# A two-layer decoder trunk on one core: the second plain pair of each gated MLP moves from the opening to the first two chained units

## The chip, the cores and the metric

The kernel runs on 1 core of one Trainium2 chip. The metric is the device time of one execution in microseconds (us); a kernel's time is the median of its runs. Engines are named as in the profile: PE (matmul), DVE (vector), ACT (scalar), POOL and SP. ACT, DVE and PE each work through their own queue in order; SP issues the loads, POOL issues transfers that add one block of SBUF onto another.

## The reference

Two layers over 512 tokens of width 1024, float32. Each layer has a token mixer (a gated recurrence with pooling in layer 0, a convolution module in layer 1), a cross-attention into 256 memory tokens, and the part that the change touches, a gated MLP with a causal depthwise convolution of width 3 on the gate branch:

```python
def conv_ffn(x, norm, w_up, dw_w, dw_b, w_down):
    h = rms_norm(x, norm) @ w_up
    g = causal_dwconv(h[..., :D_FF], dw_w, dw_b)
    u = h[..., D_FF:]
    return (jax.nn.gelu(g) * u) @ w_down
```

D_FF is 3072, so gate and value have 24 blocks of 128 columns each, "pairs" below. A final RMS norm ends the trunk.

## The kernel before, in words

Activations lie transposed: a tile has 128 channels on the partitions and 512 tokens beside them. Every float32 product is made of three matmuls on operands split into a high and a low part (`mm3`, L186 to L188): high on ACT, low on DVE. A weight piece is fetched into `raw` (ring of 3), its high part goes to `whi`, its low part to `wlo`.

The RMS norm isn't applied to x before the product. `norm.x` holds x times the gain, split; the factor of each token, `norm.r`, multiplies the product afterwards. It is one over the root of the mean of squares: `split(norm.ss)` splits the sum of squares, two matmuls (`mean_of`, L287 and L288) sum it over the channels into the bank `stat`, ACT takes the square root (L1037), and DVE the reciprocal (L1040).

The 24 pairs of a layer are made in two ways:

- The first two (`PLAIN = 2`) are plain: a gate chunk and a value chunk, each 24 matmuls of 512 tokens (`start`). `start(0)` and `start(1)` belong to pair 0, `start(2)` and `start(3)` to pair 1. `gate(c)` scales the gate chunk by `norm.r`, applies the convolution (an Identity on ACT with the middle tap, L894, and two taps on DVE, L897) and the Gelu (L899); `values(c)` multiplies by the value chunk and splits the result.
- The other 22 go through `unit(c)` for c = 2 to 23. A unit makes gate and value of one pair from seven products instead of eight of half the size (12 matmuls of 256 tokens each): with weight blocks a11, s1, s2, a12, s3, s4, a22 and operands that are the halves of `norm.x` or their sums T1 to T4. The sums come from `seven.sums(k)`, k = 0 to 3: two scaled copies on ACT (L749), four subtractions on DVE (L755 to L761), four high parts on ACT (L763) and four low parts on DVE (L766). Three of the four are made in the attention before; `sums(3)` is made in the MLP's opening.

Three PSUM accumulators serve a unit. G takes a11; ACT copies G into F (L927, the seed), and G goes on with a12, F with s2, s3 and a22. Between s2 and s3, and between s3 and a22, ACT copies F out to `u` (L946, L960); PE may write F again only after that. H takes s1 and s4. PE's order in a unit is s1, s2, a12, s3, then (from unit 4 on) 24 matmuls of the down projection, then a11 of the next pair (`ahead`), s4 and a22.

The blocks s1 to s4 don't come from memory. They are made in place in `raw` by accumulating transfers that POOL issues once a low part is done: after a11's low part `r += z` (L824), after s3's `z += a22` and `r += a22` (L827), after s2's `r += a12` (L829). The ACT row that makes s3's high part reads what the first of them left.

The order on PE, ACT, DVE and POOL is written out by hand (`manual_schedule`): it is the order of the code in `opening` and `unit`. SP's order comes from the scheduler. In `unit` the line `next(left)` takes one step of what the previous pair left over, between the unit's own steps.

`opening` computes the four plain chunks, the root and the last sums, and prepares the first units; `first` is pair 2, `second` pair 3. The down projection of six groups of four pairs is added to x in `Down`; the first down unit of a layer (c = 4) adds on DVE (`sum`), all later ones seed the bank from x on ACT (L854) and copy it home (L859).

Of the kernel before, what the change touches and what calls it, by code (L numbers as in the profile page):

```python
# [10 lines left out]
F32 = mybir.dt.float32  # L11
F32R = mybir.dt.float32r
AF = mybir.ActivationFunctionType
ALU = mybir.AluOpType
# [47 lines left out]
def trunk(ctx: ExitStack, tc: tile.TileContext, I: dict, out: list):  # L62
# [35 lines left out]
    def main_ps():  # L98
        return psum.tile([P, T], F32, tag="mm", name=nm("mm"))
# [370 lines left out]
    def attention(layer, norm, mem, nxt, six, up):  # L470
# [363 lines left out]
    def ffn(layer, norm, nxt, seven, pairs):  # L834
        ys = {}

        class Down:
# [8 lines left out]
            def products(self, i, ps, seeded=False, ks=range(GC)):  # L846
# [3 lines left out]
            def bank(self, i, seeded):  # L850

                ps = aux_ps()
                if seeded:
                    A.activation(ps, X[2 * self.j + i], AF.Copy)  # L854
                return ps

            def home(self, i, ps, seeded):
                if seeded:
                    A.activation(X[2 * self.j + i], ps, AF.Copy)  # L859
                else:  # L860
                    self.sum(i, ps)

            def sum(self, i, ps):
                n = 2 * self.j + i
# [65 lines left out]
        def unit(c):  # L930

            nonlocal left, chains
            G, F = chains
            down, seeded = downs.get(c), c > GC
# [11 lines left out]
            A.activation(u[:, :M], F, AF.Copy)  # L946
            next(left, None)
            high(c + 1, "a22")

            m(c, G, "a12", seven.B21, False)  # L950
            next(left, None)
            if down:
                d = [down.bank(i, seeded) for i in range(2)]
# [11 lines left out]
            high(c + 1, "a12")  # L965
            low(c + 1, "a12")
            if down:
                for ks in (range(GC - 1), (GC - 1,)):
                    for i in range(2):
                        down.products(i, d[i], seeded, ks)  # L970
            if c + 3 in pairs:
                pairs[c + 3].load()
            if c + 2 in pairs and c > first:
                pairs[c + 2].load_second()
            if c >= GC - 1 and c + 1 in downs:
                downs[c + 1].w.high()
                downs[c + 1].w.low()
            if c + 2 in downs and c + 2 <= CF:
                downs[c + 2].load()
            high(c + 1, "s1")  # L980
            low(c + 1, "s1")
            high(c + 1, "s2")
            low(c + 1, "s2")
            if down:
                down.home(0, d[0], seeded)

            if c + 1 in pairs:
                chains = ahead(c + 1)
            if down:
                down.home(1, d[1], seeded)  # L990
# [4 lines left out]
            next(left)  # L995

        def opening():

            nonlocal left, chains
            ps, y = {}, {}  # L1000

            def start(i, ks=range(C)):
                if ks[0] == 0:
                    ps[i] = main_ps()
                for k in ks:
                    mm3(ps[i], blk(w[0], k * P), norm.x[k], k == 0, k == C - 1)
                if ks[-1] == C - 1:
                    w.pop(0)

            def fetch(i):  # L1010
                w.append(Piece(I["wup"][(layer * 2 + i % 2) * PLAIN + i // 2]))
                w[-1].high()

            def gate(c):
                g = tmp_f()
                V.tensor_tensor(g, ps.pop(2 * c), norm.r, op=ALU.mult)
                for y[c] in gate_conv(c, g):
                    yield
                V.tensor_tensor(y[c], y[c], norm.r, op=ALU.mult)

            def values(c):
                V.tensor_tensor(y[c], ps.pop(2 * c + 1), y[c], op=ALU.mult)
                ys[c] = act_r(), act_r()
                A.activation(ys[c][0], y[c], AF.Copy)

            def close(c):
                V.tensor_tensor(ys[c][1], y[c], ys[c][0].bitcast(F32), op=ALU.subtract)
# [9 lines left out]
            A.activation(root, mean, AF.Sqrt, bias=eps)  # L1037
            A.activation(small.tile([P, 1], F32, tag="warm", name=nm("gelu"), bufs=1), eps, AF.Gelu_apprx_tanh)
            norm.r = small.tile([P, T], F32, tag="r", name=nm("r"), bufs=1)
            V.reciprocal(norm.r, root)  # L1040
# [24 lines left out]
            next(g, None)  # L1065

            start(3)
            chains = ahead(first)

            def rest():  # L1070
                values(1)
                yield
                close(1)

            left = rest()

        left, chains = None, None
        first, second = PLAIN, PLAIN + 1
# [12 lines left out]
        if nxt:  # L1091
            mem = Memory(1)
            mem.operand(0)
            mem.operand(1)
            mem.outputs()
            parked = []
            for n in range(PARKED):
                if n + 1 < C // 2:
                    downs[CF + n + 1].w = load_w(I["wdown"][(layer * NG + NG - 1) * (C // 2) + n + 1])
                parked.append(mem.key_piece(n, park=True))  # L1100
            for j in range(C // 2):
                for i in range(2):
                    ps = mm_ps()
                    downs[CF + j].products(i, ps)
                    downs[CF + j].sum(i, ps)
# [780 lines left out]
```

## Time and profile before

| | |
|---|---|
| runs | 1433.17, 1434.95, 1437.86 us, median 1434.95 |
| profiled execution | 1440.97 us, span 1439.2 us |
| granted clock of PE, mean | 0.997 |
| PE busy | 1421.0 us of the span |
| DVE, ACT, POOL busy | 1079.1, 910.2, 317.4 us |
| opening of layer 0 | first matmul at 356.65 us |
| opening of layer 1 | first matmul at 1045.94 us |

The profiled execution is one run; its own time is the span plus what lies around it. Busy times say how much an engine had to do; what sets the end is found in the waits of the engine that is nearly always busy.

### The profile page before, as it was taken

Reading aid. Unit: us, or ns where it says so; the run is one execution under the profiler, and the core shown is the slowest. Engines: PE = TensorE matmul, PEld = TensorE weight load, DVE = VectorE, ACT = ScalarE, POOL = GpSimd, SP = SyncE. Lnnn points to the kernel's source line nnn. Section 1 sums busy time; section 2 is a strip of 40 time slices with the busy share of each in tenths; the row PEclk is TensorE's granted clock in tenths of the full one; section 3 lists DMA queues with packets and bytes.
Section 4 is the critical chain, followed back from the end, with each engine's and each line's share of the span. In section 5 each row is a group of like instructions: output and inputs, shape, how many; then the busy total and the mean of one; then the engine's idle time right before and its main releaser. Section 6 shows DMA issues by size and latency. Waiting matters only on the chain.

```text
span 1439.2 us, 22840 instructions
## 1 busy us (share of the span) xinstructions
PE 1421.0 (99%) x8650; PEld 1263.3 (88%) x8650; DVE 1079.1 (75%) x1796; ACT 910.2 (63%) x1592; POOL 317.4 (22%) x333
## 2 busy tenths in 40 slices
PE   9999999999999999999999999999998999999998
PEld 8888888988999999999888777899888999999997
DVE  6987776778876666666789997877787666676665
ACT  7668755667556666666655557667654666666664
POOL 0012310100122222222009991011002222222211
PEclk9999999999999999999999999999999999999999
DMA  8522242544487777777432364345438777777751
GB/s 302 194 88 89 88 132 69 118 108 146 115 197 170 173 175 166 170 176 155 133 117 88 118 183 143 92 96 132 116 104 183 175 174 170 164 177 166 164 123 59
DMA packets 80318, 205.36 MB, mean 143 GB/s; under 512 B 9040, under 2 KB 9552, under 8 KB 80208
## 3 DMA queue, kind: packets, MB, share of 16 engines
q1 hardware_dynamic: 51120, 151.20, 34.0%
q0 software_dynamic: 28800, 52.44, 21.4%
q8 instruction: 67, 1.10, 0.3%
q14 instruction: 43, 0.35, 0.1%
q10 hardware_dynamic: 288, 0.27, 0.1%
HBM read 146.21 MB, written 2.10 MB: 103 GB/s over the span
## 4 chain that ended last, share of the span: by engine, by line
PE 82%; issue 6%; DMA 4%; DVE 3%; POOL 2%; ACT 2%; SPq 0%; POOLq 0%; DVEq 0%; ACTq 0%
PE mm L187 19%; PE mm L186 19%; PE mm L188 19%; PE aux L186 7%; PE aux L187 7%; PE aux L188 7%; PE mm L458 2%; DMA raw<-wa 1%; DMA raw<-raw 1%; DMA raw<-in_wv 1%; DMA wa<-in_wpair 1%; DVE wlo L167 1%; POOL actf L1487 1%; POOL act L167 1%; PE aux L532 1%
## 5 line engine op out<-in xcount | busy, mean ns | idle before, releaser
L186 PE MATMUL mm<-act,whi 128*128 128x512 f32 (+2 forms) x1061 | 369.2, 349 | 1.1 <-ACT whi L803 1.1
L187 PE MATMUL mm<-act,whi 128*128 128x512 f32 (+2 forms) x1061 | 369.3, 348 | 0.8 <-DVE act L181 0.4
L188 PE MATMUL mm<-act,wlo 128*128 128x512 f32 (+2 forms) x1061 | 369.0, 348 | 0.0
L186 PEld LDWEIGHTS mm<-act,whi 128*128 128x128 f32 x1061 | 200.5, 189 | 29.2 <-ACT whi L803 1.5
L187 PEld LDWEIGHTS mm<-act,whi 128*128 128x128 f32 x1061 | 200.7, 189 | 28.2 <-DVE act L167 1.0
L188 PEld LDWEIGHTS mm<-act,wlo 128*128 128x128 f32 x1061 | 200.7, 189 | 24.9 <-DVE wlo L167 0.6
L186 PE MATMUL mm<-bigr,bigr 128*128 128x256 f32 x704 | 199.8, 284 | 5.0 <-ACT tmp L946 5.0
L188 PE MATMUL mm<-bigr,bigr 128*128 128x256 f32 x704 | 199.8, 284 | 0.1
L187 PE MATMUL mm<-bigr,bigr 128*128 128x256 f32 x704 | 199.6, 284 | 0.0
L186 PE MATMUL aux<-act,whi 128*128 128x512 f32 x399 | 156.2, 391 | 0.0
L187 PE MATMUL aux<-act,whi 128*128 128x512 f32 x399 | 156.0, 391 | 0.0
L188 PE MATMUL aux<-act,wlo 128*128 128x512 f32 x399 | 155.5, 390 | 0.0
L827 POOL DMA_DIRECT2D raw<-wa x100 | 88.4, 904 | 283.9 <-DVE bigr L821 151.1
L166 ACT ACTIVATE whi<-raw 128x1024 fp32r<-128x1024 f32 (+1 forms) x95 | 96.7, 1022 | 85.9 <-PE mm L187 46.3
L814 ACT ACTIVATE bigr<-raw 128x512 fp32r<-128x512 f32 x176 | 109.5, 624 | 55.1 <-DVE wlo L203 38.5
L186 PEld LDWEIGHTS mm<-bigr,bigr 128*128 128x128 f32 x704 | 135.4, 192 | 5.6 <-ACT tmp L946 5.6
L171 DVE TENSOR_TENSOR tmp<-mm,tmp 128x256 f32<-128x256 f32 x130 | 54.0, 420 | 110.1 <-PE mm L188 109.6
L188 PEld LDWEIGHTS mm<-bigr,bigr 128*128 128x128 f32 x704 | 135.5, 193 | 0.5 <-DVE bigr L821 0.5
L187 PEld LDWEIGHTS mm<-bigr,bigr 128*128 128x128 f32 x704 | 135.4, 192 | 0.0
L821 DVE TENSOR_TENSOR bigr<-raw,bigr 128x512 fp32r<-128x512 f32 x176 | 121.0, 688 | 12.9 <-ACT bigr L814 9.5
L824 POOL DMA_DIRECT2D raw<-raw x50 | 43.3, 867 | 390.5 <-DVE wlo L821 229.8
L167 DVE TENSOR_TENSOR wlo<-raw,whi 128x1024 fp32r<-128x1024 f32 (+1 forms) x75 | 90.4, 1211 | 20.8 <-ACT whi L166 20.3
(353 smaller groups left out, 3067.5 us busy)
## 6 DMA issues: line engine op xcount, KB each, us to landing
raw<-wa POOLq DMA_DIRECT2D x150, 256.0 KB, 4.0
wa<-in_wpair SPq DMA_DIRECT2D x88, 256.0 KB, 3.8
raw<-in_wpair SPq DMA_DIRECT2D x44, 512.0 KB, 3.9
big<-in_wdown SPq DMA_DIRECT2D x44, 512.0 KB, 4.0
raw<-raw POOLq DMA_DIRECT2D x50, 256.0 KB, 5.0
raw<-in_pw SPq DMA_DIRECT2D x24, 512.0 KB, 3.3
raw<-in_win SPq DMA_DIRECT2D x20, 512.0 KB, 3.3
raw<-in_wk SPq DMA_DIRECT2D x16, 512.0 KB, 3.5
```

The lines of the kernel that those rows point to most:

```text
L166: A.activation(hi, src, AF.Copy)
L167: fetched[1] = (eng or V).tensor_tensor(lo, src, hi.bitcast(F32), op=ALU.subtract)
L171: V.tensor_tensor(out, a, b, op=ALU.add)
L186: PE.matmul(ps, wh, xh, start=first, stop=False, skip_group_check=onto)
L187: PE.matmul(ps, wh, xl, start=False, stop=False, skip_group_check=onto)
L188: PE.matmul(ps, wl, xh, start=False, stop=last, skip_group_check=onto)
L458: PE.matmul(p, m[j], x, start=k == 0 and j == 0 and x is hi, stop=k == C - 1 and x is lo)
L532: PE.transpose(pt[:, qc * P : (qc + 1) * P], es[h][qc // 2][:, j : j + P], ident)
L814: A.activation(self.w[name][0], self.block(name), AF.Copy)
L821: V.tensor_tensor(lo, self.block(name), hi.bitcast(F32), op=ALU.subtract)
L824: G.dma_start(self.r, self.z, accum_op=ALU.add)
L827: G.dma_start(block, self.a22, accum_op=ALU.add)
```

## The change

It has five parts, the same in both layers.

- `start(2)` and `start(3)`, the chunks of pair 1, leave the opening. `plain_gate` runs the first of them in unit 2 behind s3, `plain_values` the second in unit 3 behind s3, in the two banks `aux`; the steps of `gate(1)` and `values(1)` stand in these two units and the next.
- The mean's two matmuls stand after six of the eight operands of `start(0)` instead of after `start(0)` and two operands of `start(1)`.
- `seven.sums(3)` stands ahead of the square root, where it stood behind the first steps of `gate(0)`.
- The opening prepares s4 of `first` and a11 of `second`; a22 of `second` and a11 of pair 4 move into the first unit.
- The down projection always seeds its bank, at c = 4 too. One `load()` of the first down block goes, which had been issued twice. In the attention, the splits of a11 and a22 wait for the last score step.

```diff
-        prepare("a11", "a22")
+        with tc.issue_after(score.last):
+            prepare("a11", "a22")
...
-            if c == first:
-                both(c + 2, "a11")
...
             if down:
                 for ks in (range(GC - 1), (GC - 1,)):
                     for i in range(2):
-                        down.products(i, d[i], seeded, ks)
+                        down.products(i, d[i], ks)
+            if plain:
+                next(plain)
...
-            if c + 2 in pairs and c > first:
+            if c + 2 in pairs:
                 pairs[c + 2].load_second()
...
+            if plain:
+                gate1 = next(plain)
+                if c == first:
+                    plains[second] = plain_values(gate1)
...
+        def plain_gate():
+
+            start(2)
+            fetch(3)
+            w[-1].low()
+            yield
+            g = gate(1)
+            next(g)
+            yield g
+
+        def plain_values(g):
+
+            start(3)
+            for _ in g:
+                pass
+            yield
+            for _ in values(1):
+                pass
+            yield
...
             ss = split(norm.ss)
-            start(0)
-            fetch(2)
-            w[-1].low()
-            start(1, range(2))
+            start(0, range(6))
             mean = mean_of(ss)
+            start(0, range(6, C))
+            start(1)
             Norm.due = None
+            for _ in seven.sums(3):
+                pass
             root = tmp_f()
             A.activation(root, mean, AF.Sqrt, bias=eps)
...
             V.reciprocal(norm.r, root)
-            start(1, range(2, C))
+            fetch(2)
             pairs[second].load()
             pairs[second].load_second()
-            fetch(3)
             g = gate(0)
             next(g)
             w[-1].low()
-            pairs[second + 1].load()
-            pairs[second + 1].load_second()
-            downs[GC].load()
-            t = seven.sums(3, lambda: (next(g), next(g)))
-            next(t)
-            next(g, None)
-
-            start(2)
-            both(second, "a11")
-            g = gate(1)
-            next(g)
-            values(0)
-            both(second, "a22")
+            both(first, "s4")
             next(g)
             next(g)
-            next(t, None)
-            close(0)
+            both(second, "a11")
             next(g, None)
-
-            start(3)
+            pairs[second + 1].load()
             chains = ahead(first)
...
+            left = values(0)
```

In the lists below `mm` and `aux` are PSUM banks, `act` split operands, `raw` and `wa` fetched blocks, `whi` and `bigr` high or low parts, `stat` the bank of the mean; line numbers of the changed kernel differ by a few from those above.

PE, first chunk of the opening in layer 0, as a piece of the difference:

```order
 L187 MATMUL mm_700_3566<-act_647_3338,whi_694_3552 128x512
 L188 MATMUL mm_700_3566<-act_646_3337,wlo_695_3553 128x512
+L287 MATMUL stat_701_3585<-act_698_3562,ones_100 128x512
+L288 MATMUL stat_701_3585<-act_699_3563,ones_100 128x512
 L186 MATMUL mm_700_3566<-act_667_3438,whi_694_3552 128x512
 L187 MATMUL mm_700_3566<-act_668_3439,whi_694_3552 128x512
```

The two matmuls of the mean now stand inside the first chunk, behind its 18th matmul.

ACT, from the split of the sum of squares to the root and the Gelu's table, before:

```order
L166 ACTIVATE act_698_3562<-tmp_691_3546 128x512
L200 ACTIVATE whi_702_3593<-raw_701_3591 128x1024
L1037 ACTIVATE tmp_706_3607<-stat_705_3604,eps_85 128x512
L1038 ACT_TABLE_LOAD
L1038 ACTIVATE gelu_707_3609<-eps_85 128x1
```

and the same stretch of the change:

```order
L166 ACTIVATE act_698_3562<-tmp_691_3546 128x512
L750 ACTIVATE tmp_703_3619<-x_91,par_89 128x512
L750 ACTIVATE tmp_704_3620<-x_91,par_89 128x512
L764 ACTIVATE bigr_619_3236<-tmp_705_3623 128x256
L764 ACTIVATE bigr_621_3238<-tmp_706_3624 128x256
L764 ACTIVATE bigr_623_3240<-tmp_705_3623 128x256
L764 ACTIVATE bigr_625_3242<-tmp_706_3624 128x256
L1056 ACTIVATE tmp_707_3637<-stat_701_3585,eps_85 128x512
L1057 ACT_TABLE_LOAD
L1057 ACTIVATE gelu_708_3639<-eps_85 128x1
```

The six rows of the last sums moved ahead of the square root; the split of a fetched piece moved behind it.

ACT, around the first unit's seed (L927 before, L924 in the change) and its first copy to `u` (L946, L941), before:

```order
L814 ACTIVATE whi_726_3698<-raw_709_3631 128x512
L894 ACTIVATE tmp_729_3705<-tmp_728_3703,par_89 128x512
L1024 ACTIVATE act_730_3708<-tmp_716_3644 128x512
L814 ACTIVATE bigr_732_3711<-wa_710_3633 128x512
L899 ACTIVATE tmp_729_3705<-tmp_729_3705 128x512
L927 ACTIVATE mm_735_3749<-mm_734_3748 128x256
L814 ACTIVATE bigr_737_3776<-raw_709_3631 128x512
L1024 ACTIVATE act_738_3779<-tmp_729_3705 128x512
L814 ACTIVATE whi_740_3785<-raw_717_3647 128x512
L946 ACTIVATE tmp_742_3803<-mm_735_3749 128x256
```

and in the change:

```order
L891 ACTIVATE tmp_717_3656<-tmp_716_3654,par_89 128x512
L815 ACTIVATE bigr_718_3659<-raw_579_3040 128x512
L896 ACTIVATE tmp_717_3656<-tmp_717_3656 128x512
L815 ACTIVATE whi_719_3665<-raw_713_3648 128x512
L924 ACTIVATE mm_723_3674<-mm_722_3673 128x256
L815 ACTIVATE bigr_725_3701<-raw_713_3648 128x512
L1020 ACTIVATE act_726_3704<-tmp_717_3656 128x512
L941 ACTIVATE tmp_728_3723<-mm_723_3674 128x256
```

The rows that read `raw_709` before and `raw_713` now are a11 (into `whi`) and s3 (into `bigr`) of the second pair: five rows stood between them, now it is the seed alone. The Gelu ahead of the seed is pair 1's before and pair 0's now.

More of the change, by code (lines that the diff above doesn't have):

```diff
@@ L933, in unit @@
             G, F = chains
-            down, seeded = downs.get(c), c > GC
+            down, plain = downs.get(c), plains.get(c)
             H = main_ps()[:, :M]
@@ L952, in unit @@
             if down:
-                d = [down.bank(i, seeded) for i in range(2)]
+                d = [down.bank(i) for i in range(2)]
             next(left, None)
@@ L964, in unit @@
             both(c + 2, "a11")
-            high(c + 1, "a12")
-            low(c + 1, "a12")
+            both(c + 1, "a12")
             if down:
@@ L979, in unit @@
                 downs[c + 2].load()
[L980 to L983, printed above, removed]
+            both(c + 1, "s1")
+            both(c + 1, "s2")
+            if plain:
+                gate1 = next(plain)
+                if c == first:
+                    plains[second] = plain_values(gate1)
             if down:
-                down.home(0, d[0], seeded)
+                down.home(0, d[0])
             if c + 1 in pairs:
@@ L989, in unit @@
             if down:
-                down.home(1, d[1], seeded)
+                down.home(1, d[1])
             m(c, H, "s4", seven.B22, False)
@@ L995, in unit, with start, fetch @@
             next(left)
+        first, second = PLAIN, PLAIN + 1
+        ps, y = {}, {}
+        def start(i, ks=range(C)):
+            if ks[0] == 0:
+                ps[i] = aux_ps() if i > 1 else main_ps()
+            for k in ks:
+                mm3(ps[i], blk(w[0], k * P), norm.x[k], k == 0, k == C - 1)
+            if ks[-1] == C - 1:
+                w.pop(0)
+        def fetch(i):
+            w.append(Piece(I["wup"][(layer * 2 + i % 2) * PLAIN + i // 2]))
+            w[-1].high()
@@ new lines, in gate, with values @@
+        def gate(c):
+            g = tmp_f()
+            V.tensor_tensor(g, ps.pop(2 * c), norm.r, op=ALU.mult)
+            for y[c] in gate_conv(c, g):
+                yield
+            V.tensor_tensor(y[c], y[c], norm.r, op=ALU.mult)
+        def values(c):
+            V.tensor_tensor(y[c], ps.pop(2 * c + 1), y[c], op=ALU.mult)
+            ys[c] = act_r(), act_r()
+            A.activation(ys[c][0], y[c], AF.Copy)
+            yield
+            V.tensor_tensor(ys[c][1], y[c], ys[c][0].bitcast(F32), op=ALU.subtract)
@@ L997, in opening @@
+        def plain_gate():
[10 more added lines that the diff above has]
+                pass
+            yield
+            for _ in values(1):
+                pass
+            yield
         def opening():
             nonlocal left, chains
[L1000 to L1024, printed above, removed]
@@ L1047, in opening @@
             w[-1].low()
[L1048 to L1060 removed]
+            both(first, "s4")
             next(g)
             next(g)
[L1063 to L1064 removed]
+            both(second, "a11")
             next(g, None)
[L1067 removed]
+            pairs[second + 1].load()
             chains = ahead(first)
[L1070 to L1078, printed above, removed]
+            left = values(0)
+        left, chains, plains = None, None, {PLAIN: plain_gate()}
         done.update((first, name) for name in ("a11", "a22", "a12", "s3", "s1", "s2"))
@@ L1102, in ffn @@
                 for i in range(2):
-                    ps = mm_ps()
-                    downs[CF + j].products(i, ps)
-                    downs[CF + j].sum(i, ps)
+                    to = mm_ps()
+                    downs[CF + j].products(i, to, seeded=False)
+                    downs[CF + j].sum(i, to)
             return mem, parked
```

16 lines of the change are left out of this document (5 added, 11 removed).

## The prediction

> **What bounds the kernel now.** I read the page's table of engines first, then who waited for whom on PE, then one window over the second opening, then the order of time on PE, ACT, DVE and POOL around both openings (layer 0 near 356 to 406 us, layer 1 near 1046 to 1104 us). In a row of the order of time the first number is the start, the second the duration; brackets hold the idle time before it and what ended it.
>
> ```profile
> PE 1421.0 (99%) x8650; PEld 1263.3 (88%) x8650; DVE 1079.1 (75%) x1796; ACT 910.2 (63%) x1592; POOL 317.4 (22%) x333
> PE mm L186 <- ACT tmp L946: 5.0, 3, 3.7
> 1080.00:1116.00 36.00, 31.93 (x228) 30.12 (x227) 26.33 (x46) 17.73 (x33) 8.93 (x11) 0.95 0.83 184
> ```
>
> PE is the bound: 18.2 us of the 1439.2 us span are idle, and the change neither adds nor removes a matmul. Time can only move through PE's waits and its pace. The largest group of waits (5.0 us in three) is PE waiting for the copy of F in `unit` (L946), and the window of layer 1's third unit shows PE short by 4.07 us at a granted clock of 0.95. Now PE itself:
>
> ```profile
> 356.65 0.39 PE L186 MATMUL mm<-act,whi 128*128 128x512 f32 x1
> 363.45 0.39 PE L287 MATMUL stat<-act,ones 128*128 128x512 f32 x1
> 404.89 0.28 PE L187 MATMUL mm<-act,whi 128*128 128x256 f32 x1
> 405.01 0.28 PE L188 MATMUL mm<-act,wlo 128*128 128x256 f32 x1
> 406.45 0.39 PE L186 MATMUL mm<-bigr,bigr 128*128 128x256 f32 x1 [1.16 <-ACT tmp L946]
> ...
> 1045.94 0.39 PE L186 MATMUL mm<-act,whi 128*128 128x512 f32 x1
> 1051.44 0.50 PE L187 MATMUL mm<-act,whi 128*128 128x512 f32 x1 [0.29 <-DVE act L223]
> 1074.95 0.39 PE L186 MATMUL mm<-bigr,bigr 128*128 128x256 f32 x1 [0.22 <-ACT tmp L946]
> 1088.54 0.39 PE L186 MATMUL mm<-act,bigr 128*128 128x256 f32 x1 [0.37 <-DVE tmp L171]
> 1095.99 0.28 PE L188 MATMUL mm<-act,wlo 128*128 128x256 f32 x1
> 1099.93 0.39 PE L186 MATMUL mm<-bigr,bigr 128*128 128x256 f32 x1 [3.67 <-ACT tmp L946]
> 1100.51 0.41 PE L187 MATMUL mm<-bigr,bigr 128*128 128x256 f32 x1
> 1102.21 0.63 PE L186 MATMUL aux<-act,whi 128*128 128x512 f32 x1
> 1103.92 0.40 PE L187 MATMUL aux<-act,whi 128*128 128x512 f32 x1
> ```
>
> Rows 356.65 and 363.45 are the first matmul of the opening and the mean's, 30 matmuls apart: a 512-wide one costs 0.227 us of pace; a 256-wide one costs 0.12 (404.89 to 405.01). So `start` of one chunk (24 matmuls) covers 5.44 us, one block of a unit (12 matmuls) 1.44 us.
>
> **What can be won.** Layer 0: the third unit's wait, 405.01 to 406.45 less the pace, 1.32 us. Layer 1: the same wait, 1095.99 to 1099.93, 3.82 us; half pace behind it (eight 256-wide matmuls from 1100.51 to 1102.21 take 1.70 instead of 0.96, four 512-wide to 1103.92 take 1.71 instead of 0.91), 1.54 us; and the three short waits 0.29 + 0.22 + 0.37. Together 1.32 + 6.24 = 7.56 us. The remaining waits lie outside the openings, and nothing there changes but one split (below).
>
> **What the change adds.** It takes two chunks, 10.88 us of PE work, from the opening and puts 5.44 us each into units one and two. That work was the cover under which ACT, DVE and a POOL transfer got the first unit ready. The durations:
>
> ```profile
> 361.30 0.63 ACT L166 ACTIVATE act<-tmp 128x512 fp32r<-128x512 f32 x1 [0.96 <-DVE tmp L231]
> 364.17 0.69 ACT L1037 ACTIVATE tmp<-stat,eps 128x512 f32<-128x512 f32 x1 [1.28 <-PE stat L288]
> 369.13 0.82 ACT L894 ACTIVATE tmp<-tmp,par 128x512 f32<-128x512 f32 x1 [0.65 <-DVE tmp L1016]
> 369.86 1.33 ACT L749 ACTIVATE tmp<-x,par 128x512 f32<-128x512 f32 x2
> 371.71 0.63 ACT L899 ACTIVATE tmp<-tmp 128x512 f32<-128x512 f32 x1 [0.53 <-DVE tmp L897]
> 372.33 1.37 ACT L763 ACTIVATE bigr<-tmp 128x256 fp32r<-128x256 f32 x4
> 373.60 0.62 ACT L814 ACTIVATE whi<-raw 128x512 fp32r<-128x512 f32 x1
> 380.52 0.37 ACT L927 ACTIVATE mm<-mm 128x256 f32<-128x256 f32 x1 [0.18 <-PE mm L188]
> 1052.08 0.63 ACT L166 ACTIVATE act<-tmp 128x512 fp32r<-128x512 f32 x1 [0.96 <-DVE tmp L231]
> 1098.46 0.63 ACT L814 ACTIVATE bigr<-raw 128x512 fp32r<-128x512 f32 x1 [4.33 <-DMA raw<-raw]
> ```
> ```profile
> 361.96 0.69 DVE L167 TENSOR_TENSOR act<-tmp,act 128x512 fp32r<-128x512 f32 x1 [0.76 <-ACT act L166]
> 364.89 3.35 DVE L1040 RECIPROCAL r<-tmp 128x512 f32<-128x512 f32 x1 [0.75 <-ACT tmp L1037]
> 368.35 0.69 DVE L1016 TENSOR_TENSOR tmp<-mm,r 128x512 f32<-128x512 f32 x1
> 368.95 1.22 DVE L203 TENSOR_TENSOR wlo<-raw,whi 128x1024 fp32r<-128x1024 f32 x1
> 370.09 1.53 DVE L897 SCALAR_TENSOR_TENSOR tmp<-tmp,par,tmp 128x511 f32<-128x511 f32 x2
> 371.54 0.42 DVE L755 TENSOR_TENSOR tmp<-tmp,tmp 128x256 f32<-128x256 f32 x1
> 374.25 0.69 DVE L821 TENSOR_TENSOR wlo<-raw,whi 128x512 fp32r<-128x512 f32 x1 [0.56 <-ACT whi L814]
> 1052.74 0.69 DVE L167 TENSOR_TENSOR act<-tmp,act 128x512 fp32r<-128x512 f32 x1 [0.76 <-ACT act L166]
> ```
> ```profile
> 375.24 0.86 POOL L824 DMA_DIRECT2D raw<-raw  x1 [27.54 <-DVE wlo L821]
> 378.81 0.86 POOL L827 DMA_DIRECT2D raw<-wa  x1 [2.71 <-DMA raw<-raw]
> raw<-raw POOLq DMA_DIRECT2D x50, 256.0 KB, 5.0
> ```
>
> *The mean.* PE meets it after 18 matmuls: 356.65 + 18 x 0.227 = 360.73. Its operands, the split of the sum of squares, stand behind unchanged work and end at 361.93 (ACT) and 362.65 (DVE), so PE waits; in layer 1 it arrives at 1045.94 + 4.08 = 1050.02 against 1053.43. This wait is not a term of its own: the next one starts later by as much and ends at a time that PE doesn't set.
>
> *The root and the first copy of F, layer 0.* After 361.93 ACT now runs `sums(3)`: two copies (1.33) to 363.17; DVE's subtractions start at 363.26; the four high parts end 2.16 later (371.54 to 373.70 in the rows), 365.42; the square root 366.01; the reciprocal 366.10 to 369.45, 1.2 later than now. Then one chain over two queues: `g` from 369.56, the low part of the fetched weights (0.60 and 1.22) to 371.38; on ACT the Identity ends 371.16, s4's high part 371.68, on DVE its low part 372.45; two taps to 373.90; Gelu 373.99 to 374.62; the second pair's a11 high 375.14; and only then the copy of G into F, 375.41, on which s2 of the first unit waits until 375.46. PE alone would be there after two chunks, the mean, a11 and s1: 356.65 + 10.88 + 0.45 + 2.88 = 370.86. Term: 4.60 us, the mean's wait within. In layer 1 the chain hangs on 1053.43 instead of 362.65: s2 at 1066.24, against 1045.94 + 14.21 = 1060.15; term 6.09. Every row of the chain is measured, and each step needs the one before it or stands behind it on its queue, so I see no lower end than some tenths.
>
> *The high part of s3.* Before, a11's low part (374.25) and the ACT row that reads the accumulated block lie 6 us apart, with two chunks of PE work between. Now a11's low part runs 375.23 to 375.92, POOL issues at 376.22, and the next row on ACT behind the copy is s3's high part, which reads that block. The transfer took 375.24 to 378.81 = 3.57 us; so ACT goes on at 379.79, s3 to 380.42, the plain chunk's copy 380.94, the copy of u (s2's result) 381.21. Queued behind this one wait are all of ACT's rows, DVE's low parts, and PE: s2 and a12 end at 378.34, s3 starts at 381.26. Term: 2.92 us a layer. The page's median landing of 5.0 us is the upper end, 4.35; the lower is zero, if PE came later by other means. I take 3.57, the row of the same transfer at the same place of the opening.
>
> *Units two and three.* With 5.44 us of matmuls after s3 of the first unit ACT and DVE catch up, and I find no wait in unit two. There the second chunk's own steps (scale, two taps, two products, low part: about 4.2 us of DVE by the rows) fall on a full queue; walked on, the third unit's copy of u ends at 413.3, while PE has done a12 at 412.3. Term: 1.1 us, with ends 0 and today's 3.82. The long wait of layer 1 (row 1098.46: ACT stood 4.33 us for an accumulation) has more room, since 5.44 us more lie between issue and use.
>
> *The rest at nothing.* The first down products now seed two banks and copy them home on ACT (8 copies in all) for 4 DVE additions; ACT is the less loaded of the two (63% against 75% in the page's first row). A second load of the same `wdown` block goes (2 x 512 KB); none of PE's waits above names it. One split (a22) leaves the score stage for later; PE's waits there name other tiles. If this cover were gone the seed could cost 0.3 us a layer.
>
> *Clock.* After 3.67 us idle PE ran at half pace; after 1.16 us it didn't. The new gaps, near 2.9 us, lie between. I take no loss; the upper end is 1.54 each. The Trainium skill's page "TensorE: Matmul & The Clock Gate", Part 1: The HAM clock gate, says that PE's clock is halved after an idle window of about 3.4 us that runs freely, and the trace agrees at 3.67 us. By that rule gaps of 2.9 us stay free, and the sum is the same; those of 4.35 us would pay.
>
> **Sum.** New: 4.60 + 2.92 + 1.1 in layer 0, 6.09 + 2.92 + 1.1 in layer 1, 18.7. Won: 7.56. Net +11.2 us, half of it before the first unit's s2. Against the profiled execution (1440.97, span 1439.2 and 1.8 around it) that is 1452. That execution lies 6.0 above the median of the runs, 1434.95, and above their highest; on the median the same sum gives 1446.
>
> **Rivals.**
> - *The chunks beside the units pay and the opening holds* (other side): the copy of F stands in time in both layers, and so does s3. It decides where ACT ends that copy by 371.2 instead of 375.4 in layer 0. For it: 7.56 us of waits are real, and the first two units are where PE has least to do. Against it: reciprocal and taps alone take 4.9 us. 1434.95 - 7.6 = 1427.
> - *Only the root's chain costs*: accumulation and third unit are covered. 10.7 - 7.6 = +3.1: 1438, within the noise.
> - *The accumulation lands late and the clock falls*: 1.43 more for each s3 wait and 1.54 behind it, +5.9: 1452. For it: the window's DMA share of 0.83 and the 5.0 median.
> - *Layer 1's long wait belongs to the profiled run*: if the timed runs wait there as layer 0 does, 2.50 + 1.54 less is won: 1450. For it: the profiled run is 6 us long.
>
> **How the numbers follow.** The forecast's own case has 0.50, late accumulation 0.20, the profiled run's wait 0.15, only the root's chain 0.10, the other side 0.05. A change within 0.3% (4.3 us) can't be told from none here: slower 0.85, same 0.10, faster 0.05. The range runs from just under the smallest loss, 1437, to the two larger cases with the third unit's upper end in part, 1455.
>
> **What would show it.** PE idle in two pieces before the stat matmuls; then about 2.9 us before the first unit's s2, released by the copy of G; about 2.9 us before its s3, released by the copy of u, with ACT idle for an accumulation just ahead; near 1 us in the third unit, and no half pace. I am wrong if PE goes into the first s2 without a wait, or if the third unit's waits stay while the new ones come.

## The result, and the profile after

| | before | the change |
|---|---|---|
| runs, median (lowest to highest) | 1435.47 us (1433.17 to 1437.86), 4 runs | 1449.87 us (1447.31 to 1452.29), 4 runs |
| profiled execution, span | 1440.97, 1439.2 us | 1449.17, 1447.4 us |
| granted clock of it | 0.997 | 0.996 |

The ratio is 1.0100, with a 95% interval of 1.0075 to 1.0125: the change costs 14.4 us. The forecast was 1446, 11.2 above the median of before as it stood then (1434.95), with a range from 1437 to 1455.

The profile of the changed kernel, read as the one before: first the table of engines, then who waited for whom on PE (total, times, longest).

```profile
PE 1423.2 (98%) x8650; PEld 1265.9 (87%) x8650; DVE 1077.3 (74%) x1792; ACT 912.8 (63%) x1600; POOL 316.8 (22%) x333
```
```profile
PE mm L186 <- ACT tmp L941: 6.6, 4, 2.6
PE stat L287 <- ACT act L166: 4.0, 2, 2.9
PE mm L186 <- ACT mm L924: 3.2, 2, 2.4
```

PE has the same 8650 matmuls and 2.2 us more of busy time. The waits have changed place: the mean (L287), the first unit's s2, held up by the copy of G into F (L924), and the copies of F into `u` (L941), which now are the first unit's s3 and the third unit's. Here is PE in order of time, layer 0 and then layer 1; the first row of each is the first matmul of the opening.

```profile
354.58 0.39 PE L186 MATMUL mm<-act,whi 128*128 128x512 f32 x1
359.89 0.51 PE L287 MATMUL stat<-act,ones 128*128 128x512 f32 x1 [1.07 <-ACT act L166]
373.23 0.58 PE L186 MATMUL mm<-bigr,bigr 128*128 128x256 f32 x1 [2.40 <-ACT mm L924]
380.37 0.58 PE L186 MATMUL mm<-bigr,bigr 128*128 128x256 f32 x1 [2.52 <-ACT tmp L941]
383.50 0.39 PE L187 MATMUL aux<-act,whi 128*128 128x512 f32 x1
413.75 0.39 PE L186 MATMUL mm<-bigr,bigr 128*128 128x256 f32 x1 [0.70 <-ACT tmp L941]
...
1051.07 0.39 PE L186 MATMUL mm<-act,whi 128*128 128x512 f32 x1
1058.21 0.49 PE L287 MATMUL stat<-act,ones 128*128 128x512 f32 x1 [2.90 <-ACT act L166]
1071.54 0.39 PE L186 MATMUL mm<-bigr,bigr 128*128 128x256 f32 x1 [0.80 <-ACT mm L924]
1077.31 0.39 PE L186 MATMUL mm<-bigr,bigr 128*128 128x256 f32 x1 [2.63 <-ACT tmp L941]
1109.35 0.39 PE L186 MATMUL mm<-bigr,bigr 128*128 128x256 f32 x1 [0.70 <-ACT tmp L941]
```

Without a wait s2 would start 14.21 us behind the opening's first matmul. It starts at 373.23 - 354.58 = 18.65 and 1071.54 - 1051.07 = 20.47: 4.44 and 6.26 us late. From s2 to s3 lie 24 matmuls, 2.88 us; it took 7.14 and 5.77, so s3 comes 4.26 and 2.89 us later still. The 3.67 us that layer 1's third unit waited before have gone.

What PE waits for is seen on the other three engines, in layer 0 and, for the accumulation, in layer 1 too:

```profile
359.21 0.63 ACT L166 ACTIVATE act<-tmp 128x512 fp32r<-128x512 f32 x1 [0.96 <-DVE tmp L231]
...
368.15 0.82 ACT L891 ACTIVATE tmp<-tmp,par 128x512 f32<-128x512 f32 x1 [1.85 <-DVE tmp L1012]
371.75 0.63 ACT L896 ACTIVATE tmp<-tmp 128x512 f32<-128x512 f32 x1 [2.26 <-DVE tmp L894]
372.29 0.61 ACT L815 ACTIVATE whi<-raw 128x512 fp32r<-128x512 f32 x1
372.81 0.36 ACT L924 ACTIVATE mm<-mm 128x256 f32<-128x256 f32 x1
378.90 0.63 ACT L815 ACTIVATE bigr<-raw 128x512 fp32r<-128x512 f32 x1 [5.72 <-DMA raw<-raw]
379.95 0.36 ACT L941 ACTIVATE tmp<-mm 128x256 f32<-128x256 f32 x1
...
1075.83 0.63 ACT L815 ACTIVATE bigr<-raw 128x512 fp32r<-128x512 f32 x1 [4.35 <-DMA raw<-raw]
```
```profile
363.92 3.35 DVE L1059 RECIPROCAL r<-tmp 128x512 f32<-128x512 f32 x1
370.13 1.53 DVE L894 SCALAR_TENSOR_TENSOR tmp<-tmp,par,tmp 128x511 f32<-128x511 f32 x2
```
```profile
373.93 0.86 POOL L825 DMA_DIRECT2D raw<-raw  x1 [28.30 <-DVE wlo L822]
1072.24 0.86 POOL L825 DMA_DIRECT2D raw<-raw  x1 [28.45 <-DMA raw<-in_wup]
```

The chain is the one walked in the prediction: split, reciprocal (3.35), scale, Identity, taps, Gelu (371.75), a11's high part (372.29), seed (372.81). The Identity and the Gelu wait for DVE; the two rows behind the Gelu follow it on ACT without a wait. Behind the seed ACT stands 5.72 us for an accumulation, which POOL issued at 373.93 and which had landed when the row started at 378.90 (4.97 us); in layer 1 the same row on ACT starts at 1075.83, 3.59 us behind the issue at 1072.24. No engine is overloaded in this time: the window around s3 of the first unit, one row for each layer, shows ACT and DVE idle for more than half of it in layer 0 and for a third to a half in layer 1 (busy us of each engine, granted clock, DMA share, GB/s).

```profile
376.00:386.00 10.00, 7.48 (x38) 6.78 (x38) 4.53 (x9) 4.60 (x9) 2.18 (x3) 0.80 0.48 91
1074.00:1084.00 10.00, 7.37 (x41) 6.28 (x40) 6.72 (x11) 5.35 (x10) 2.58 (x3) 1.00 0.62 115
```

The clock is 0.80 in the first and 1.00 in the second. The two executions that were profiled lie 8.2 us apart, less than the medians: before's is 5.5 above its median, the change's 0.7 below. Of the 8.2, the opening of layer 0 starts 2.07 earlier than before (354.58 against 356.65), layer 1's starts 5.13 later (1051.07 against 1045.94), and the end comes 8.2 later. A row in between divides this further: the first matmul of L298, in layer 1's mixer, starts at 844.77 before and at 852.07 now. So the stretch from layer 0's opening to that row is 9.37 us longer, the stretch from it to layer 1's opening 2.17 shorter, and the stretch from there to the end 3.07 longer. (One remark on the first unit: a11 of pair 4 is made in it in both kernels, before behind s1, now behind s3.)

### The profile page after: what moved, and what is told of

The parts are those of the page before. It is cut to its first block, busy times and chain, and to the rows that moved or that the text cites. A ratio compares the mean times of both kernels' runs of the same rounds, so it can differ in the third digit from the quotient of the medians.

```text
span 1447.4 us, 22826 instructions
## 1 busy us (share of the span) xinstructions
PE 1423.2 (98%) x8650; PEld 1265.9 (87%) x8650; DVE 1077.3 (74%) x1792; ACT 912.8 (63%) x1600; POOL 316.8 (22%) x333
## 4 chain that ended last, share of the span: by engine, by line
PE 84%; DVE 6%; issue 3%; ACT 2%; DMA 2%; POOL 2%; SPq 0%; POOLq 0%; DVEq 0%; ACTq 0%
PE mm L186 20%; PE mm L187 20%; PE mm L188 20%; PE aux L186 7%; PE aux L187 7%; PE aux L188 7%; PE mm L458 2%; DMA raw<-in_wv 1%; DVE wlo L167 1%; DMA raw<-raw 1%; POOL actf L1484 1%; DVE wlo L203 0%; PE aux L532 0%; ACT whi L166 0%; POOL act L167 0%
## 5 line engine op out<-in xcount | busy, mean ns | idle before, releaser
L187 PE MATMUL mm<-act,whi 128*128 128x512 f32 (+2 forms) x1029 | 357.7, 348 | 0.5 <-DVE act L181 0.4
L186 PE MATMUL mm<-act,whi 128*128 128x512 f32 (+2 forms) x1029 | 357.5, 348 | 0.0
L188 PE MATMUL mm<-act,wlo 128*128 128x512 f32 (+2 forms) x1029 | 357.3, 347 | 0.0
L187 PEld LDWEIGHTS mm<-act,whi 128*128 128x128 f32 x1029 | 195.3, 190 | 26.5 <-DVE act L167 1.0
L186 PEld LDWEIGHTS mm<-act,whi 128*128 128x128 f32 x1029 | 195.1, 190 | 26.5 <-ACT tmp L1483 0.8
L188 PEld LDWEIGHTS mm<-act,wlo 128*128 128x128 f32 x1029 | 195.3, 190 | 23.9 <-DVE wlo L167 0.6
L186 PE MATMUL aux<-act,whi 128*128 128x512 f32 x431 | 168.6, 391 | 0.0
L187 PE MATMUL aux<-act,whi 128*128 128x512 f32 x431 | 168.2, 390 | 0.0
L188 PE MATMUL aux<-act,wlo 128*128 128x512 f32 x431 | 167.7, 389 | 0.0
```

Of the source, the lines that this page charges most:

```text
L186: PE.matmul(ps, wh, xh, start=first, stop=False, skip_group_check=onto)
L187: PE.matmul(ps, wh, xl, start=False, stop=False, skip_group_check=onto)
L188: PE.matmul(ps, wl, xh, start=False, stop=last, skip_group_check=onto)
```

## The experiments

My theory: the loss is the order of the rows on ACT behind the sum of squares, that is, the seed behind the Gelu's chain and s3's high part behind an accumulation issued too late; where the mean stands, and where the second pair's chunks stand, costs nothing by itself. The rivals: the mean's wait is a cost of its own; the chunks in the units are the cost; the small parts (attention split, second load, seeding) are. The kernels of the first four experiments below ran on one chip (before there: 1436.94, 1433.96 to 1441.67, 19 runs), the other four on another (before there: 1436.23, 1434.05 to 1441.67, 21 runs); a ratio is always to before on the same chip.

### The mean back in its old place

```diff
-            start(0, range(6))
-            mean = mean_of(ss)
-            start(0, range(6, C))
-            start(1)
+            start(0)
+            start(1, range(2))
+            mean = mean_of(ss)
+            start(1, range(2, C))
```

> The changed kernel with one thing undone: the mean's two matmuls stand again behind 30 matmuls instead of 18. Theory (one chain over ACT and DVE sets when the first unit's s2 may start, PE's idle before the mean is only a part of that wait seen early): the two gaps before the stat matmuls go (1.5 us in layer 0, 3.3 us in layer 1), the gap before s2 grows by about as much, and the time stays where the changed kernel's is, 1450 within 2 us; a longer gap may cost half pace. Rival (each gap on PE is a cost of its own): 4.8 us less than the changed kernel, 1445, with the gap before s2 unchanged at 2.4 us in layer 0.

Measured: 1448.5 us (1447.56 to 1453.4), ratio 1.0091 (1.0076 to 1.0106). The waits on PE:

```profile
PE mm L186 <- ACT mm L924: 9.4, 2, 5.1
PE mm L186 <- ACT tmp L941: 6.9, 4, 2.8
```

No row for the mean is left, and the wait of s2 has grown from 3.2 to 9.4 us in two. The time is that of the change, by overlapping intervals. s2 starts 18.65 and 20.16 us behind the opening's first matmul (373.40 - 354.75 and 1072.74 - 1052.58), where it was 18.65 and 20.47 in the change. So the mean's wait is no cost of its own: what PE saves there it waits at the seed.

### The first unit's a11 and seed ahead of the gate's chain

```diff
+            chains = ahead(first)
             g = gate(0)
             next(g)
             w[-1].low()
             both(first, "s4")
...
-            chains = ahead(first)
```

> The changed kernel with the first unit's seed (the copy of G into F) put ahead of pair 0's Identity, Gelu and the second pair's a11 on ACT. Theory: the gap before s2 goes (2.4 us in layer 0, 0.8 in layer 1 of the changed kernel), but s3's high part on ACT still waits for the accumulation that hangs on the reciprocal's chain, so the gap before the first unit's s3 grows to about 5.5 us and the time stays near the changed kernel's, 1450 within 2 us, with half pace behind the long gap. Rival (the place of the seed alone is at fault): 3 to 6 us less, 1445.

Measured: 1453.68 us (1452.24 to 1454.98), ratio 1.0122 (1.0106 to 1.0137): not better than the change, rather a little worse, and above the 1450 within 2 us that I had expected. PE, both layers, and what ACT and POOL do in layer 0:

```profile
380.71 0.58 PE L186 MATMUL mm<-bigr,bigr 128*128 128x256 f32 x1 [6.55 <-ACT tmp L941]
1077.99 0.58 PE L186 MATMUL mm<-bigr,bigr 128*128 128x256 f32 x1 [6.56 <-ACT tmp L941]
```
```profile
369.88 0.37 ACT L924 ACTIVATE mm<-mm 128x256 f32<-128x256 f32 x1 [3.10 <-PE mm L188]
370.16 0.81 ACT L891 ACTIVATE tmp<-tmp,par 128x512 f32<-128x512 f32 x1
374.29 0.61 ACT L815 ACTIVATE whi<-raw 128x512 fp32r<-128x512 f32 x1
379.24 0.63 ACT L815 ACTIVATE bigr<-raw 128x512 fp32r<-128x512 f32 x1 [4.33 <-DMA raw<-raw]
```

The wait of s2 is gone and stands at s3, with 6.55 us. The seed itself now waits 3.10 us for PE, and the Identity behind it comes 2.0 us later than in the change (370.16 against 368.15; 0.5 of this is the later start of the opening); a11's high part still follows the Gelu, and the accumulation follows that. So the order that binds is a11 of the second pair behind the Gelu, with the transfer behind it. To move the seed alone only moves the wait: s3 starts 25.67 and 26.80 us behind the opening's first matmul (355.04 and 1051.19), against 25.79 and 26.24 in the change. What is worse than the change is the pace: behind s3 PE ran at half pace until 384.25 and 1083.70, about 1.7 and 2.8 us by the pace of the same matmuls, where the change paid 1.46 us in layer 0 alone.

### The second pair's a11 ahead of the sum of squares

```diff
+            pairs[second].load()
+            pairs[second].load_second()
+            both(second, "a11")
             ss = split(norm.ss)
...
             fetch(2)
-            pairs[second].load()
-            pairs[second].load_second()
...
-            both(second, "a11")
             next(g, None)
```

> The changed kernel with the second pair's load and its a11 split put ahead of the split of the sum of squares, where ACT and DVE stand idle, so that the accumulation starts some 13 us earlier. Theory: the gap before the first unit's s3 (2.5 us in layer 0, 2.6 in layer 1) goes, and the seed comes 0.5 us earlier, so 3 us a layer and what half pace cost: 6 to 9 us less than the changed kernel, 1442 within 2. Rival (PE is held by the reciprocal's chain through other rows of ACT anyway): under 2 us less, 1448 to 1450, with a gap of the same size before s3 released by the plain pair's steps.

Measured: 1441.18 us (1438.61 to 1442.58), ratio 1.0027 (1.0016 to 1.0038). That is 7.3 us under the first experiment's kernel by the medians of the same chip, and some 10 under the change by the ratios (1.0027 against 1.0100). POOL, the row on ACT that waited, and PE at the first unit's s2 in layer 0:

```profile
358.27 0.86 POOL L825 DMA_DIRECT2D raw<-raw  x1 [12.24 <-DVE wlo L822]
```
```profile
372.62 0.37 ACT L924 ACTIVATE mm<-mm 128x256 f32<-128x256 f32 x1
372.92 0.61 ACT L815 ACTIVATE bigr<-raw 128x512 fp32r<-128x512 f32 x1
```
```profile
373.04 0.39 PE L186 MATMUL mm<-bigr,bigr 128*128 128x256 f32 x1 [1.90 <-ACT mm L924]
```

POOL issues 15.7 us earlier, s3's high part follows the seed without a wait, and PE has no wait at s3. By the rows of the change s3 cost 4.26 + 2.89 us, and the half pace behind it in layer 0 another 1.46 (12 matmuls of 0.12 and one of 0.227 took 383.50 - 380.37 = 3.13): 8.6 in all. That is the accumulation's share. s2 also comes 0.6 and 1.4 us sooner, 18.07 and 19.02 behind the opening's first matmul (373.04 - 354.97 and 1063.88 - 1044.86); the two together are 10.6, what the ratios show. The mean's and the seed's waits are still there: s2 is late by 3.9 and 4.8 us, and the kernel is still 0.27% over before.

### The small parts on the kernel before

Three parts without the move: the bank always seeded, the second load of the down block dropped, the attention's split behind the last score. (Seeded in this way the kernel doesn't give the reference's result; it counts for its time only.)

```diff
-        prepare("a11", "a22")
+        with tc.issue_after(score.last):
+            prepare("a11", "a22")
...
-            downs[GC].load()
...
-            down, seeded = downs.get(c), c > GC
+            down, seeded = downs.get(c), True
```

> The kernel before with the small parts of the change alone: the down bank always seeded, the second load of the first down block dropped, the attention's splits of a11 and a22 behind the last score. The opening keeps its four plain chunks. Theory: within 0.3% of before, 1435.5 within 3 us; its profile is also a second look at the third unit's wait of before in layer 1, which the first profile showed as 3.67 us: if it is near 1.2 us here, the long wait belonged to that one execution. Rival (the small parts carry a good part of the loss): 3 us or more above before.

Measured: 1433.49 us (1431.98 to 1437.83), ratio 0.9984 (0.9973 to 0.9996). The same without the seeding, so with the two other parts alone:

> The kernel before with two small parts of the change alone: the second load of the first down block dropped and the attention's splits behind the last score; the down bank as before. Theory: the small gain of the run with three small parts comes from the load and the split, so 1434 within 2 us, and layer 1's third unit waits 1.2 to 1.6 us. Rival (the seeded bank carried it): 1436 to 1438.

Measured: 1432.84 us (1430.74 to 1437.36), ratio 0.9976 (0.9964 to 0.9988): a gain of 0.24%, 3.4 us (1.7 to 5.2). The gain is there without the seeding, so the seeded bank isn't what brings it. It is small and real, and I had put these parts at nothing. The trace of before shows a price: the rows of PE and ACT in the score stage of layer 1.

```profile
971.55 0.39 PE L186 MATMUL mm<-act,whi 128*128 128x256 f32 x1 [0.42 <-ACT whi L803]
972.28 0.39 PE L188 MATMUL mm<-act,whi 128*128 128x256 f32 x1 [0.22 <-DVE whi L821]
```
```profile
969.18 0.63 ACT L814 ACTIVATE bigr<-wa 128x512 fp32r<-128x512 f32 x1 [3.55 <-DMA wa<-in_wpair]
970.88 0.62 ACT L803 ACTIVATE whi<-raw 128x512 fp32r<-128x512 f32 x1
```

The a22 split waited 3.55 us for its load, and the part that PE waited for stood behind it on ACT. The prediction said that PE's waits in the score stage name other tiles; they do, but the queue behind the split goes through those tiles. With 0.66 + 0.22 in layer 0 these waits come to 1.5 us; neither kernel in which the split stands later has them. The rest lies ahead of the openings too: layer 0's opening starts at 355.35 and 355.63 us in these two kernels, against 356.65 before, and from the first matmul of L298 in layer 1's mixer to layer 1's opening PE takes 198.7 us in both (843.63 to 1042.36, 843.15 to 1041.84), against 201.17 before. That is 3.7 and 3.5 us. The split stands in these stages; but at a second row of L298 in layer 1's mixer PE waits 1.70 us for DVE before, and 0.8 and 0.7 in these two, which the split doesn't explain. Before has only one trace, and no run has the split alone, so how much of the gain is the split's stays open. The third unit of these two kernels, whose opening is that of before, in layers 0 and 1:

```profile
405.11 0.39 PE L186 MATMUL mm<-bigr,bigr 128*128 128x256 f32 x1 [1.12 <-ACT tmp L947]
1093.41 0.39 PE L186 MATMUL mm<-bigr,bigr 128*128 128x256 f32 x1 [1.44 <-ACT tmp L947]
```
```profile
405.05 0.39 PE L186 MATMUL mm<-bigr,bigr 128*128 128x256 f32 x1 [0.78 <-ACT tmp L947]
1094.56 0.39 PE L186 MATMUL mm<-bigr,bigr 128*128 128x256 f32 x1 [2.27 <-ACT tmp L947]
```

The wait of 3.67 us in layer 1 is not what this opening always shows. The 2.27 us is outside the 1.2 to 1.6 that I had expected; that execution took 1436.4 us, 3.6 above the median of its kernel.

### The chunks beside the units, with the opening in another order

The change's place for the chunks, with four things moved: the mean in its old place and a11 first (both as above), the seed ahead of the gate's chain, and in the first unit the copy of F to `u` ahead of s3's high part and of the Gelu of pair 0.

```diff
             m(c, H, "s1", seven.T1)
-            high(c + 1, "s3")
+            if c != first:
+                high(c + 1, "s3")
             next(left, None)
-            low(c + 1, "s3")
+            if c != first:
+                low(c + 1, "s3")
...
             A.activation(u[:, :M], F, AF.Copy)
+            if c == first:
+                both(c + 1, "s3")
...
+            chains = ahead(first)
             g = gate(0)
             next(g)
             w[-1].low()
             both(first, "s4")
             next(g)
-            next(g)
-            both(second, "a11")
-            next(g, None)
             pairs[second + 1].load()
-            chains = ahead(first)
-            left = values(0)
+            left = rest(g)
```

`rest(g)` gives the unit the gate's last steps (taps and Gelu) and then those of `values(0)`, one step at each `next(left)`.

> The changed kernel with its opening put in another order, the plain chunks still beside units two and three of the pairs: a11 of the second pair ahead of the sum of squares, the mean behind 30 matmuls, the seed ahead of pair 0's Identity, and in the first unit the copy of u ahead of s3's high part and of pair 0's Gelu. Theory (the loss is the order on ACT, not the place of the chunks): PE goes through the opening and the first unit without a wait over 0.5 us in either layer, only the third unit's wait near 0.9 us stays, and the time is 13 to 17 us under the changed kernel, 1434 within 3 us. Rival (two chunks less of cover can't carry the reciprocal and the weights' splits at all): gaps of 2 us or more come up elsewhere, at the plain chunk or at the second unit's s1, and the time stays above 1440.

Measured: 1431.64 us (1430.1 to 1433.57), ratio 0.9961 (0.9946 to 0.9975). ACT in layer 0, and PE's only group of waits in the openings and the first three units that is over 0.3 us; it stands in the third unit:

```profile
368.25 0.37 ACT L924 ACTIVATE mm<-mm 128x256 f32<-128x256 f32 x1 [1.31 <-PE mm L188]
371.19 0.39 ACT L943 ACTIVATE tmp<-mm 128x256 f32<-128x256 f32 x1 [1.06 <-PE mm L188]
372.40 0.63 ACT L896 ACTIVATE tmp<-tmp 128x512 f32<-128x512 f32 x1 [0.30 <-DVE tmp L894]
```
```profile
PE mm L186 <- ACT tmp L943: 1.5, 2, 0.8
```

Now ACT waits for PE, at the seed and at the copy to `u`, and the Gelu comes behind both. The same chunks in the same units with the same matmuls: 0.4% under before, where the change is 1% over it. The chunks' place is not the cost.

### The third unit's copy ahead of the pair before

On the two small parts alone (before's opening), and on the reordered opening, in the third unit:

```diff
-            next(left, None)
             u, f, g = tmp_f(), tmp_f(), tmp_f()
+            if c != second + 1:
+                next(left, None)
             A.activation(u[:, :M], F, AF.Copy)
+            if c == second + 1:
+                next(left, None)
```

> The kernel of the two small parts, and in the third unit the copy of u ahead of the previous pair's Gelu on ACT. Theory: the third unit's wait (1.3 us in layer 0, 1.6 or more in layer 1) hangs on that Gelu and goes, 2 to 3 us less than the run of the two small parts, 1431 within 2 us. Rival (the third unit is held by an accumulation on ACT ahead of the Gelu): no change, a wait of the same size released by the same copy.

> The reordered opening, and in the third unit the copy of u ahead of the previous pair's Gelu. Theory: the last wait near 0.9 us a layer goes, 1.5 to 2 us less than the reordered opening alone, 1432 within 3 us. Rival: the wait only passes to the next copy in the same unit, no change.

Measured: on before's opening 1431.4 us (1429.89 to 1434.12), ratio 0.9963 (0.9948 to 0.9979), and no wait is recorded in the third unit any more. On the reordered opening 1430.89 us (1429.95 to 1432.37), ratio 0.9958 (0.9941 to 0.9974); there the copy's wait is gone too, but the down product behind it waits for the copy of x into its bank instead, as the rival had it:

```profile
PE aux L186 <- ACT aux L854: 1.9, 2, 1.0
```

The times don't show a gain from this step: the intervals overlap with those of the kernels without it (0.9976 and 0.9961), and the 2 to 3 and 1.5 to 2 us that I had expected are not measured. These two and the reordered opening can't be told apart. They all beat both kernels, by 0.4% of before, and before's opening with small edits does it as well as the chunks beside the units. So the move itself brings nothing that can be measured here.

## Why the prediction was right

The mechanism was right: every wait that it named is there, in its place and with its releaser. By its terms, in us:

| term | forecast, layer 0, 1 | measured |
|---|---|---|
| s2 late, the mean's wait within | 4.60, 6.09 | 4.44, 6.26 |
| s3 late | 2.92, 2.92 | 4.26, 2.89 |
| third unit (with pace) | 1.1, 1.1 | 0.86, 0.86 |
| half pace behind s3 | 0, 0 | 1.46, 0 |
| sum | 18.7 | 21.0 |

- *The root and the copy of F.* Right to 0.2 us, because each row of the chain had its duration and releaser in the trace of before. That the mean's wait is no term was argued there; the first experiment showed it.
- *The high part of s3.* Right in layer 1 (the transfer took 3.59, forecast 3.57), too small in layer 0 (4.97). The forecast's upper end, 5.0, is what came. The third experiment showed the price of both.
- *The clock.* "No loss" was mis-sized: PE ran at half pace behind gaps of 2.40 and 2.52 us in layer 0 and 2.90 in layer 1. Two of the three lie ahead of a wait that takes them up (behind the gap of 2.40 PE idles for s3 in any case; behind the mean in layer 1, for the seed), so of these only the 1.46 us behind s3 are paid. The rival of the late accumulation with a falling clock was thus half true: in layer 0, not in layer 1.
- *What is won.* 7.56 us was the loss of the profiled execution. It doesn't hold for the others: of the 40 runs of before made beside the experiments, 39 show a granted clock of 0.998 to 1.000 where the profiled one had 0.997, and two kernels with the same opening waited 1.44 and 2.27 us in layer 1, the second with half pace behind it. The rival "the long wait belongs to the profiled run" was partly true.
- *The rest at nothing.* Mis-sized by 3.4 us (1.7 to 5.2), a gain. At least 1.5 us of it was to be seen in the trace; I read the names of the tiles PE waited for, not what stood ahead of them on ACT.
- *The second unit.* No wait was forecast and none is there.

The two profiled executions fit these sums. By the terms the change costs 11.0 - 1.32 = 9.7 us in layer 0, and the stretch from its opening to layer 1's mixer grew by 9.37; in layer 1 the terms give 10.0 - 6.24 = 3.8, and the stretch from its opening to the end grew by 3.07. Ahead of the two openings it gains 2.07 and 2.17 us, where the prediction had nothing.

For the median, with 21.0 new and 3.4 won by the small parts, a loss of 3.2 us in the openings of a usual run of before, in place of 7.56, would give the measured 14.4. The 3.2 is what is left over, not a measurement. It fits the third-unit waits of the two kernels with its opening (1.12 + 1.44 and 0.78 + 2.27), but the intervals of the ratios, 2 to 4 us wide on each side, don't allow to say more. So three sizes were off: 2.3 us too little new cost, 3.4 of gain left out, and about 4.4 too much counted as won. The second of these errors went against the other two. That the forecast's 11.2 came within 3.2 us of the result is in part luck; that the waits stood where they were forecast is not.

## What to carry to other kernels

On an engine that works in order, the matmuls of an opening are the cover for the whole chain of rows that runs beside them: before they are moved, walk the chain row by row with the durations of the trace, through every queue it crosses, and ask which rows could stand ahead of the chain instead (here the split that a transfer waits for). Moving one waiting row alone, or the wait ahead of it, only hands the wait on, as the first two experiments and the last show. A wait in a single profiled execution is not yet what the median pays, and a row that PE waits for may be late because of the row ahead of it, which has another name.

## What the hardware showed that I had not expected

PE's half pace doesn't follow the length of the gap alone. Gaps of 2.40 and 2.52 us (layer 0) and 2.90 (layer 1) were followed by it, while 2.63 us in layer 1 was not; here is the second matmul behind the gap of 2.40, the first at full pace again there, the first that is nearly so behind the gap of 2.90, and the second matmul behind that of 2.63.

```profile
373.61 0.42 PE L187 MATMUL mm<-bigr,bigr 128*128 128x256 f32 x1
376.60 0.30 PE L186 MATMUL mm<-act,whi 128*128 128x256 f32 x1
...
1062.65 0.42 PE L188 MATMUL mm<-act,wlo 128*128 128x512 f32 x1
1077.53 0.28 PE L187 MATMUL mm<-bigr,bigr 128*128 128x256 f32 x1
```

In layer 0 the pace came back at 376.60 and 383.50, 6.9 us apart, and in layer 1 at about 1062.65. The Trainium skill's page "TensorE: Matmul & The Clock Gate", Part 1: The HAM clock gate, says that the clock is decided in free-running windows of 3413 ns. The two returns in layer 0 agree with it (6.9 is 2.02 such windows). By an estimate with that figure, window edges in layer 1 lie at 1062.65 + 4 x 3.41 = 1076.30, so that the gap of 2.63 us (1074.68 to 1077.31) falls into two windows, while that of 2.40 us (370.83 to 373.23) ends at an edge, 376.60 - 3.41 = 373.19, and lies in one. If that reading holds, a window need not be idle throughout: 2.40 us of idle time were enough. In another trace the fall comes well behind the gap: in the kernel of the two small parts PE resumes at 1094.56, after its gap of 2.27 us, at full pace, falls to half pace some 0.9 us later and is back near 1098.74.

```profile
1094.78 0.28 PE L187 MATMUL mm<-bigr,bigr 128*128 128x256 f32 x1
1095.54 0.42 PE L187 MATMUL mm<-bigr,bigr 128*128 128x256 f32 x1
```

In the prediction I had read the rule as "under 3.4 us stays free", which the runs don't bear out.

The accumulating transfer of 256 KB, issued by the same line at the same place of the opening, took 3.59 us in one layer and 4.97 in the other; in the traces of the first two experiments it took 5.1 and 5.3, and twice 3.3, from issue to landing. It is a price with a spread, and a chain that hangs on it should be costed at both ends.
